# A product of quarters for the sixth of seven products, with its operands kept in DRAM

## The chip, the cores and the metric

The kernel runs on one core of a Trainium2 chip. The time is the device time of one execution in microseconds (us); the median of three runs counts. The engines of a core work side by side, each through its own list of instructions in a fixed order, and wait for each other by semaphores: TensorE (PE; its weight loads are shown as PEld), VectorE (DVE), ScalarE (ACT), GpSimd (POOL) and SyncE (SP). POOL and SP do nothing here but issue DMA transfers. All transfers of the core run on the same 16 DMA engines; SP's requests go through the queue that the profile calls q1, POOL's through q0.

## The reference

```python
def setup_inputs():
    m, k, n = 4096, 4096, 4096
    return {
        "a": np.random.randn(m, k).astype(np.float32),
        "b": np.random.randn(k, n).astype(np.float32),
        "alpha": np.float32(0.01),
    }

def reference(a: np.ndarray, b: np.ndarray, alpha: np.float32) -> np.ndarray:
    x = np.matmul(a, b)
    return np.where(x > 0, x, alpha * x)
```

A product of two 4096 x 4096 matrices and a leaky ReLU on the result.

## The kernel before

**Regions.** The result is cut into 4 x 4 regions of 1024 x 1024. A region (g, j) is group g of rows and block j of columns. The first, (0, 0), is computed plainly while data comes in. The other fifteen are run by the loop at L665, in the order (0, 1), (0, 2), (0, 3), (1, 2), (1, 0), (1, 1), (1, 3), (2, 2), (2, 0), (2, 3), (2, 1), (3, 2), (3, 0), (3, 1), (3, 3). The inputs are rounded to 16-bit floats on their way into the chip's memory (SBUF); sums are kept in 32 bits.

**Seven products instead of eight.** In a region, a's rows and b's columns are each two halves of 512, and the inner dimension two halves of 2048. The 2 x 2 blocks are multiplied by Winograd's form of Strassen's method: seven products (`PRODUCTS`, numbered 0 to 6 in the code) of sums of blocks. They are, in order, a11 b11; a12 b21; s2 t2; s3 t3; s1 t1; a22 (b21 - t2); s4 b22. The texts call a22 (b21 - t2) the sixth and s4 b22 the seventh. s1 to s4 are sums of blocks of a and serve all regions of a group; t1 to t3 are sums of blocks of b, made by VectorE on b's own tiles in each region (`b_sum`, L561). b's tiles are addressed as (half, nt, k): half of the inner dimension, half of the columns, and k, which halves the inner half again. b22 is (1, 1); it enters t2 and t3, and so the operand of the product s2 t2, as the sum `B(0, 1, k) = b22 - b12` and then `B(0, 0, k)`.

A whole product is 64 matmuls of 128 x 128 by 128 x 512 (L680) into four banks of PSUM. PSUM has eight banks; a region uses four as y (products 0, 2, 4, 5 or 6) and four as z. ScalarE copies banks into tiles `c` (`keep`), VectorE adds banks to them (`add`), applies the leaky ReLU (L307), and SP stores them (`leave`, L740).

**A product in quarters.** In nine regions (`in_quarters`: group above 0, not the last of its group) the seventh product is itself cut into 2 x 2 and made of seven products of quarters (`quarters_product`): seven times 16 matmuls of 128 x 128 by 128 x 256 (L711). This needs four sums of quarters of s4 (made once per group by `sums_s4`, kept in DRAM as `kept_s`, and loaded again in the two other regions) and four of b22 (made by VectorE in each region, `sums_b`, L644 to L647).

**Space.** `x_pool` has three slots of 2 MB. s1, s2 and s4 live there; since the sums of quarters need a slot, s2 is given up after its product, comes from DRAM (`kept_s2`) at the region's end, and lies there for the next. s3 overwrites a21 in `a_pool`. `a16_pool` has three slots of 0.5 MB, for a's pieces on their way in, for squares that are measured, and for sums of quarters.

**Loads of b.** Each region's b is 8 MB in 16-bit floats. The next region's tiles go where this region's lie, as soon as the products have read them: `fetch_b(i + 1, ...)` for (0, 1), (0, 0), (1, 0) and (1, 1) in this order, in halves by k, each half by two DMAs of 512 KB from POOL (L505). In the first region of a group b comes from a rounded copy in DRAM, by SP. In the last of a group (`turning`) the next group's a is loaded too (L130) and turned by VectorE (L139).

**Squares.** The kernel measures the sizes of the blocks (`Measure`, placed by `MEASURED` and `EARLY`): ScalarE squares, VectorE adds and folds. At the end this decides whether the fast method's result stands, or all is computed anew.

**Order.** Tiles and their waits are set by the framework; the order on each engine is the order of the code. Places that matter below: `u1 = keep(y, side)` and the four `b_sum` after product 0, `add(u1, z)` after product 1, `in_quarters` after product 3, `add(v, y)` and `leave(v, 1, 1)` after product 4, `product(5, z, False)` with `add(u2, z)`, and `quarters_product` at the end. SP's queue follows the same order: a request whose slot isn't free holds those behind it.

Of the kernel before, what the change touches and what calls it, by code (L numbers as in the profile page):

```python
# [8 lines left out]
P = 128  # L9
DT = mybir.dt.float16  # L10
# [14 lines left out]
KC = 8  # L25
# [6 lines left out]
MT = 4  # L32
# [14 lines left out]
def kernel(  # L47
# [526 lines left out]
    def judge():  # L574
# [26 lines left out]
    B11, B12, B21, B22 = ((1, half, nt) for half in range(2) for nt in range(2))  # L601
    MEASURED = {
        (0, 1): (None, [A11], B12, B11), (0, 2): (B21, [B22, A22], B12, A12),
        (1, 2): (None, [A11], None, None), (1, 0): (B21, [B22, A12], None, None),
        (1, 1): (B21, [B22, A22], None, None),
        (2, 2): (None, [A11], None, None), (2, 0): (A12, [], None, None),
        (2, 3): (B21, [B22, A22], None, None),
        (3, 2): (None, [A11], None, None), (3, 0): (A12, [A22], None, None),
    }


# [3 lines left out]


    HALF = NT // 2
    kept_s = dram_pool.tile([4, P, KC * HALF], DT, name="kept_s")
    kept_s2 = dram_pool.tile([P, 2 * KC * RM], DT, name="kept_s2")
    side = 0  # L620

    def quarter_a(t):
        return t.rearrange("p (c m e) -> p c m e", m=HALF, e=2)

    def rooms(i):

        two = x_pool.tile([P, 2, 2, KC * HALF], DT, name="q", tag="x")
        two = [two[:, 0], two[:, 1]]
        three = [a16_pool.tile([P, KC * HALF], DT, name="sq4", tag="a16") for _ in range(3)]
        tq = {2: two[0][:, 0], 1: two[0][:, 1], 4: two[1][:, 0]}  # L630
        sq = {1: three[0], 2: three[1], 3: three[2], 4: two[1][:, 1]}
        return tq, sq

    def quarters_b(i):
        return {(k, n): have_b[i, 2 + k, 1][:, :, n * HALF:(n + 1) * HALF] for k in range(2) for n in range(2)}

    def quarters_s4(g):
        return {(h, k): s[g, "s4", k][:, :, h * HALF:(h + 1) * HALF, :] for h in range(2) for k in range(2)}

    def sums_b(i, tq):  # L640
        y = quarters_b(i)
        f = lambda n: tq[n].rearrange("p (c n) -> p c n", n=HALF)
        tt = nc.vector.tensor_tensor
        tt(y[0, 1], y[1, 1], y[0, 1], SUB)  # L644
        tt(f(2), y[0, 1], y[0, 0], ADD)
        tt(f(1), y[1, 1], f(2), SUB)
        tt(f(4), y[1, 0], f(2), SUB)  # L647

    def sums_s4(g, sq):
        x = {key: q.rearrange("p c m e -> p c (m e)") for key, q in quarters_s4(g).items()}  # L650
        f = lambda n: sq[n].rearrange("p (c m) -> p c m", m=2 * HALF)
        tt = nc.vector.tensor_tensor
        tt(f(1), x[1, 0], x[1, 1], ADD)
        tt(f(2), f(1), x[0, 0], SUB)
        tt(f(3), x[0, 0], x[1, 0], SUB)
        tt(f(4), x[0, 1], f(2), SUB)
        for n in range(4):
            nc.sync.dma_start(kept_s[n], sq[n + 1])


    def next_a(g, h, half):
# [3 lines left out]
    for i, (g, j) in enumerate(regions):  # L665
# [19 lines left out]
        def new_c(side):  # L685

            pairs = [c_pool.tile([P, 2, NT], FP32, name="c", tag=f"c{side}") for _ in range(2)]
            return pairs, [pairs[mt // 2][:, mt % 2, :] for mt in range(MT)]

        def keep(banks, side):  # L690
            _, kept = new_c(side)
            for mt in range(MT):
                nc.scalar.copy(kept[mt], banks[mt])  # L693
            return kept

        def quarters_product(i, y, acc, other, tq, sq):

            pairs, kept = new_c(side)
            block = lambda r, n: pairs[r][:, :, n * HALF:(n + 1) * HALF]
            b = quarters_b(i)  # L700
            x = quarters_s4(g)
            f = lambda n: tq[n].rearrange("p (c n) -> p c n", n=HALF)
            into = lambda bank: [bank[:, m * HALF:(m + 1) * HALF] for m in range(2)]
            onto = lambda r, n: [y[2 * r + m][:, n * HALF:(n + 1) * HALF] for m in range(2)]
            pair = lambda bank: bank.rearrange("p (m n) -> p m n", m=2)

            def part(xq, yq, to, first=False):
                for c in range(KC):
                    for m in range(2):
                        rows = slice(m * P, (m + 1) * P)  # L710
                        nc.tensor.matmul(  # L711
                            to[m], xq[:, c // 2, rows, c % 2], yq[:, c, :],
                            start=first and (c, m) == (0, 0), stop=c == KC - 1, skip_group_check=True,
                        )

            part(x[0, 1], b[1, 0], onto(0, 0))
            part(x[0, 0], b[0, 0], into(acc), True)
            nc.scalar.copy(block(0, 0), pair(acc))  # L718
            part(quarter_a(sq[4]), b[1, 1], onto(0, 1))
            part(quarter_a(sq[2]), f(2), into(acc))  # L720
            nc.scalar.copy(block(0, 1), pair(acc))
            part(quarter_a(sq[1]), f(1), into(other), True)
            nc.vector.tensor_add(block(0, 1), pair(other), block(0, 1))
            part(quarter_a(sq[3]), b[0, 1], into(acc))
            for n in (1, 0):
                nc.scalar.copy(block(1, n), pair(acc))
            nc.vector.tensor_add(block(1, 1), pair(other), block(1, 1))
            part(x[1, 1], f(4), onto(1, 0))
            for mt in range(MT):
                nc.vector.tensor_add(kept[mt], y[mt], kept[mt])  # L730
            return kept
# [5 lines left out]
        def leave(acc, h, nt):  # L737
            for mt in range(MT):
                leaky(acc[mt])
                nc.sync.dma_start(place(g, h, mt, j, nt), acc[mt])  # L740
# [14 lines left out]
        def fetch_a(h, half, some=slice(None)):  # L755
            if turning:
                for fetch, turn in coming[h, half][some]:
                    fetch()
                    turn()
# [5 lines left out]
        late_ones = [measure(i, *x) for x in late_ones]  # L765
        first_of_group = i == 0 or regions[i - 1][0] != g
        in_quarters = g > 0 and not turning and not final
        early = measure(i, *EARLY[g, j]) if (g, j) in EARLY else None
        if early:
            early.begin()  # L770
        if first_of_group and g:
            nc.sync.dma_start(kept_s2, whole_s[g, "s2"].rearrange("p k c m e -> p (k c m e)"))

        product(0, y, True)
        if early:
            early.end()
        if middle:
            middle.begin()
        u1 = keep(y, side)
        for k in range(2):  # L780
            b_sum(B(0, 1, k), B(1, 1, k), B(0, 1, k), SUB)
            b_sum(B(0, 0, k), B(0, 1, k), B(0, 0, k), ADD)
        if middle:
            middle.end()
        fetch_a(0, 0)

        product(1, z, True)
        add(u1, z)
        if first_of_group:
            sum_a(g, "s3")  # L790
        leave(u1, 0, 0)
        for k in range(2):
            b_sum(B(1, 0, k), B(1, 0, k), B(0, 0, k), SUB)
# [3 lines left out]
        product(2, y, False)  # L797
        if late_ones:
            late_ones[0].begin()
        u2 = keep(y, 1 - side)  # L800
        for k in range(2):
            b_sum(B(0, 0, k), B(1, 1, k), B(0, 0, k), SUB)
        if g:
# [5 lines left out]

        z = [new_bank(zbank + mt) for mt in range(MT)]  # L810
        product(3, z, True)
        v = keep(z, side)
        fetch_b(i + 1, [(0, 1)])
        fetch_a(1, 0)
        for m in late_ones[1:]:
            m.begin()
            m.end()
        if in_quarters:
            tq, sq = rooms(i)
            if first_of_group:  # L820
                sums_s4(g, sq)
            else:
                for n in (4, 2, 1, 3):
                    nc.sync.dma_start(sq[n], kept_s[n - 1])
            if len(late_ones) < 2:
                sums_b(i, tq)

        product(4, y, False)
        a21 = None
        if turning:  # L830
            new_s(g + 1, "s1")
            t = new_s(g + 1, "s2").rearrange("p k c m e -> p (k c m e)").bitcast(BF16)
            a21 = measure(i + 1, 0, 1, 0, t.rearrange("p (n w) -> p n w", n=4))
            a21.begin()
        add(v, y)
        leave(v, 1, 1)
        if in_quarters and len(late_ones) == 2:
            sums_b(i, tq)
        if a21:
            a21.end()  # L840
        if fifth:
# [4 lines left out]
        if final:  # L846
            good = judge()

        product(5, z, False)
        fetch_b(i + 1, [(1, 0)])  # L850
        add(u2, z)
        fetch_a(1, 1, slice(3))
        leave(u2, 1, 0)
        if sixth:
# [6 lines left out]
                sum_a(g + 1, name)  # L861

        if in_quarters:
            kept_c = quarters_product(i, y, new_bank(zbank + 2), new_bank(zbank + 3), tq, sq)
            fetch_b(i + 1, [(1, 1)])
            t = new_s(g, "s2")
            nc.sync.dma_start(t.rearrange("p k c m e -> p (k c m e)"), kept_s2)
            leave(kept_c, 0, 1)
        else:
            product(6, y, False)  # L870
            fetch_b(i + 1, [(1, 1)])
            if final:
                even = nc.values_load(good[0:1, 0:1], min_val=0, max_val=1)
            _, kept_c = new_c(side)

            def store(mt):
                nc.sync.dma_start(place(g, 0, mt, j, 1), kept_c[mt])

            for mt in range(MT):
                nc.scalar.copy(kept_c[mt], y[mt])  # L880
                leaky(kept_c[mt])
                if not (final and mt == MT - 1):
                    store(mt)
# [69 lines left out]
```

## Time and profile before

| what | value |
|---|---|
| median of 3 runs | 1567.9 us (1567.63 to 1568.17) |
| the profiled execution | 1567.84 us |
| its span in the profile | 1565.9 us |
| granted TensorE clock | 0.999 |
| instructions in the profile | 19332 |
| moved by DMA | 291.84 MB, 186 GB/s over the span |

The profile is of one execution. Its page gives each engine's busy time and share of the span, DMA queues with packets, megabytes and the time that their packets took as a share of 16 engines' span, and the costliest groups of instructions. Other views give the instructions in order of time (start, length, engine, line, operation, output and inputs, and in brackets the idle time before and what ended it) and the busy time by stage. A DMA share over 1 means that packets overlapped on the engines. Regions start, by PE's timeline, at 412.93 (1, 2), 508.03 (1, 0), 603.14 (1, 1), 698.25 (1, 3), 794.94 (2, 2), 890.05 (2, 0), 985.15 (2, 3), 1080.26 (2, 1), 1176.95 (3, 2), 1272.06 (3, 0), 1367.16 (3, 1) and 1462.27 (3, 3).

### The profile page before, as it was taken

To read this page: it belongs to the slowest core of one execution; us is meant where nothing else is said; L and a number is where in the kernel's file an instruction comes from. 1 tells how busy PE (TensorE), PEld (TensorE's weight loads), DVE (VectorE), ACT (ScalarE), POOL (GpSimd) and SP (SyncE) were. 2 spreads that over 40 slices of the span, in tenths; PEclk is the share of its full clock that TensorE was granted. 3 is DMA by queue.
4 is the path that set the end of the run, shared out by engine and by line. 5 is a ranking of instruction groups with operands and counts; after the bars stand their busy time and mean duration, and the time that the engine had idled before them with its cause. 6 is when DMAs were issued, how large, how long until landed. Compare 5 with 4: busy or idle time off the path is not lost. (4 is left out here: it accounts for less than half of the span.)

```text
span 1565.9 us, 19332 instructions
## 1 busy us (share of the span) xinstructions
PE 1554.8 (99%) x7707; PEld 753.0 (48%) x7707; DVE 1055.6 (67%) x1172; ACT 372.4 (24%) x390; POOL 299.7 (19%) x482
## 2 busy tenths in 40 slices
PE   9999999999999999999999999999999999999998
PEld 4444444444445445454444545545444454544543
DVE  4378758767975776766789682774868959372533
ACT  2201243612120334401221220531022143110110
POOL 5641110244002011023401102012330110201100
PEclk9999999999999999999999999999999999999999
DMA  9999795999829589499975949769995793949902
GB/s 244 186 217 185 151 279 150 190 194 203 284 54 246 157 167 237 92 249 209 183 275 114 276 135 174 176 140 276 168 235 203 170 260 96 217 144 193 210 27 84
DMA packets 199142, 291.84 MB, mean 186 GB/s; under 512 B 17281, under 2 KB 154753, under 8 KB 193666
## 3 DMA queue, kind: packets, MB, share of 16 engines
q0 software_dynamic: 149376, 141.59, 57.4%
q1 hardware_dynamic: 49378, 148.53, 25.4%
q8 instruction: 62, 1.02, 0.3%
q10 hardware_dynamic: 288, 0.39, 0.1%
q14 instruction: 38, 0.31, 0.1%
HBM read 341.84 MB, written 88.08 MB: 275 GB/s over the span
## 5 line engine op out<-in xcount | busy, mean ns | idle before, releaser
L680 PE MATMUL ps<-b,a 128*128 128x512 f16 x3840 | 836.1, 379 | 0.0
L680 PEld LDWEIGHTS <-a 128*128 128x128 f16 x3840 | 375.7, 98 | 451.1
L680 PE MATMUL ps<-b,s 128*128 128x512 f16 x2304 | 503.2, 379 | 0.0
L680 PEld LDWEIGHTS <-s 128*128 128x128 f16 x2304 | 225.4, 98 | 271.9
L561 DVE TENSOR_TENSOR b<-b 128x4096 f16<-128x4096 f16 x112 | 252.8, 2290 | 94.9 <-DMA b<-in_b_dram 80.0
L505 POOL DMA_DIRECT2D b<-in_b_dram x184 | 136.3, 746 | 940.9 <-PE ps L680 635.7
L735 DVE TENSOR_TENSOR c<-ps,c 128x512 f32<-128x512 f32 x180 | 111.6, 683 | 168.4 <-PE ps L680 110.1
L693 ACT COPY c<-ps 128x512 f32<-128x512 f32 x180 | 92.3, 598 | 538.5 <-PE ps L680 431.0
L139 DVE STREAM_TRANSPOSE a<-a 128x512 uint32<-128x512 uint32 (+2 forms) x120 | 126.3, 1101 | 90.5 <-DMA a<-in_a_dram 89.8
L130 POOL DMA_DIRECT2D a<-in_a_dram x252 | 137.5, 553 | 196.5 <-DVE a L139 122.5
L307 DVE SCALAR_TENSOR_TENSOR c<-c 128x512 f32<-128x512 f32 x240 | 149.5, 686 | 12.7 <-ACT c L880 10.0
L227 ACT ACTIVATE sq<-b 128x2048 bf16<-128x2048 f16 x64 | 119.1, 1910 | 89.8 <-DVE sq L236 75.8
L279 PE MATMUL ps<-b,a 128*128 128x512 f16 x512 | 112.8, 379 | 2.1 <-DMA b<-in_b_dram 0.9
L227 ACT ACTIVATE sq<-a 128x2048 bf16<-128x2048 f16 x48 | 88.8, 1921 | 77.2 <-DVE sq L236 60.3
L279 PEld LDWEIGHTS <-a 128*128 128x128 f16 x512 | 49.7, 98 | 63.0 <-issue 2.9
L718 ACT COPY c<-ps 128x512 f32<-128x512 f32 x9 | 5.3, 586 | 244.2 <-PE ps L711 244.2
L236 DVE TENSOR_TENSOR sq<-sq 128x2048 bf16<-128x2048 bf16 x27 | 33.0, 1223 | 28.8 <-ACT sq L227 28.8
L711 PEld LDWEIGHTS <-s 128*128 128x128 f16 x432 | 42.2, 98 | 6.8
L239 DVE TENSOR_TENSOR sq<-sq 128x2048 bf16<-128x2048 bf16 x27 | 33.1, 1225 | 17.2 <-ACT sq L227 17.2
L711 PEld LDWEIGHTS <-sq 128*128 128x128 f16 x432 | 42.3, 98 | 4.8
L238 DVE TENSOR_TENSOR sq<-sq 128x2048 bf16<-128x2048 bf16 x27 | 33.1, 1226 | 4.7 <-ACT sq L227 2.3
L880 ACT COPY c<-ps 128x512 f32<-128x512 f32 x24 | 12.6, 598 | 98.0 <-PE ps L680 98.0
(86 smaller groups left out, 559.7 us busy)
## 6 DMA issues: line engine op xcount, KB each, us to landing
b<-in_b_dram POOLq DMA_DIRECT2D x192, 512.0 KB, 10.5
out_dram<-c SPq DMA_DIRECT2D x240, 256.0 KB, 6.5
a<-in_a_dram POOLq DMA_DIRECT2D x244, 128.0 KB, 5.5
b<-kept SPq DMA_DIRECT2D x24, 1024.0 KB, 8.5
s<-kept_s SPq DMA_DIRECT2D x9, 2048.0 KB, 10.4
sq<-kept_s SPq DMA_DIRECT2D x18, 512.0 KB, 7.1
b<-in_b_dram POOLq DMA_DIRECT2D x24, 256.0 KB, 9.2
kept<-b SPq DMA_DIRECT2D x6, 1024.0 KB, 7.7
```

The costliest lines, as they stand in the source:

```text
L130: nc.gpsimd.dma_start(a16[32 * q:32 * q + 32], src.rearrange("(g i) w -> i g w", i=32))
L139: nc.vector.transpose(part.rearrange("p c m e -> p c (m e)").bitcast(U32) .rearrange("p c (g i) -> p g c i", i=32), src[:, :, i * n:(i + 1 ...
L227: nc.scalar.activation(to, self.parts[n], SQUARE)
L238: nc.vector.tensor_add(total, total, more[1])
L279: nc.tensor.matmul(ps, a_cols(at[0, h, u], c, mt, (h, u) == (0, 0)), bt[0, u, nt][:, c, :], start=first, stop=last,)
L307: nc.vector.scalar_tensor_tensor(t, t, alpha, t, op0=MULT, op1=MAX if alpha <= 1 else MIN)
L505: nc.gpsimd.dma_start(t[:, c:c + 4, :], b_rows(j, u, c, 4, nt, g > 0))
L561: nc.vector.tensor_tensor(f(to), f(x0), f(x1), op)
L680: nc.tensor.matmul(banks[mt], a_cols(t, c, mt, t is first_a), B(half, nt, k)[:, c, :], start=first and (k, c) == (0, 0), stop=(k, c) == (1 ...
L693: nc.scalar.copy(kept[mt], banks[mt])
L711: nc.tensor.matmul(to[m], xq[:, c // 2, rows, c % 2], yq[:, c, :], start=first and (c, m) == (0, 0), stop=c == KC - 1, skip_group_check=True,)
L735: nc.vector.tensor_add(acc[mt], banks[mt], acc[mt])
```

## The change

In six regions, those `in_quarters` that are not the first of their group (`both`: (1, 0), (1, 1), (2, 0), (2, 3), (3, 0), (3, 1)), the sixth product is formed from seven products of quarters as well. The space for its sums is made by keeping s1 and s3 in DRAM too, beside s2: they are written in the group's first region, given up in each of the six, and loaded again at its end. a22's sums of quarters are made in the group's first region and kept in DRAM. Where the sixth product was added into z, on top of s3 t3, it now has banks of its own, and v (a copy of z) is added to u2 before. The blocks whose squares are measured are dealt out to other regions.

```diff
     MEASURED = {
         (0, 1): (None, [A11], B12, B11), (0, 2): (B21, [B22, A22], B12, A12),
-        (1, 2): (None, [A11], None, None), (1, 0): (B21, [B22, A12], None, None),
-        (1, 1): (B21, [B22, A22], None, None),
-        (2, 2): (None, [A11], None, None), (2, 0): (A12, [], None, None),
-        (2, 3): (B21, [B22, A22], None, None),
+        (1, 0): (A12, [B22], None, None), (1, 1): (A22, [A11], None, None),
+        (2, 0): (B21, [A12], None, None), (2, 3): (A22, [A11], None, None),
         (3, 2): (None, [A11], None, None), (3, 0): (A12, [A22], None, None),
+        (3, 1): (B21, [B22], None, None), (3, 3): (B21, [B22], None, None),
     }
...
-    kept_s = dram_pool.tile([4, P, KC * HALF], DT, name="kept_s")
-    kept_s2 = dram_pool.tile([P, 2 * KC * RM], DT, name="kept_s2")
+    QUARTER = KC * HALF
+    kept_s = {name: dram_pool.tile([P, 2 * KC * RM], DT, name=f"kept_{name}") for name in ("s1", "s2", "s3")}
+    kept_q = {name: dram_pool.tile([4, P, QUARTER], DT, name=f"kept_q{name}") for name in ("a22", "s4")}
...
+    def load_sums(name, to, which):
+        for n in which:
+            nc.sync.dma_start(to[n], kept_q[name][n - 1])
+
+    def quarter_product(xq, yq, to, first=False):
+        for c in range(KC):
+            for m in range(2):
+                rows = slice(m * P, (m + 1) * P)
+                nc.tensor.matmul(
+                    to[m], xq[:, c // 2, rows, c % 2], yq[:, c, :],
+                    start=first and (c, m) == (0, 0), stop=c == KC - 1, skip_group_check=True,
+                )
...
+    def load_s(g, name):
+        if name == "s3":
+            for k in range(2):
+                t = s[g, name, k] = a_pool.tile([P, KC // 2, RM, 2], DT, name="s3", tag="a21")
+                nc.sync.dma_start(t.rearrange("p c m e -> p (c m e)"), kept_s[name][:, k * KC * RM:(k + 1) * KC * RM])
+        else:
+            t = new_s(g, name)
+            nc.sync.dma_start(t.rearrange("p k c m e -> p (k c m e)"), kept_s[name])
...
+        def sixth_in_quarters(pairs, banks, tq, sq, w):
+            b = quarters_of_b(i, 1, 0)
+            x = quarters_of_a(g, "a22")
+            one, other, third, fourth = banks
...
+            quarter_product(x[0, 0], b[0, 0], into(one), True)
+            nc.scalar.copy(w[0], one)
+            quarter_product(sx(1), t(1), into(other), True)
+            more(1, 1, other)
+            quarter_product(x[0, 1], b[1, 0], into(fourth), True)
+            quarter_product(sx(2), t(2), into(one))
+            nc.scalar.copy(w[1], one)
+            quarter_product(x[1, 1], t(4), into(third), True)
+            quarter_product(sx(3), b[0, 1], into(one))
+            quarter_product(sx(4), b[1, 1], into(other))
+            yield
+            more(0, 0, fourth)
+            more(0, 0, w[0])
+            more(0, 1, w[1])
+            more(1, 0, third)
+            more(1, 0, one)
+            more(1, 1, one)
+            more(0, 1, other)
...
         in_quarters = g > 0 and not turning and not final
+        both = in_quarters and not first_of_group
...
         if in_quarters:
-            tq, sq = rooms(i)
-            if first_of_group:
-                sums_s4(g, sq)
-            else:
-                for n in (4, 2, 1, 3):
-                    nc.sync.dma_start(sq[n], kept_s[n - 1])
-            if len(late_ones) < 2:
-                sums_b(i, tq)
+            t = x_pool.tile([P, 4, QUARTER], DT, name="q", tag="x")
+            tq, sq = {2: t[:, 0], 1: t[:, 1], 4: t[:, 2]}, {4: t[:, 3]}
+        if both:
+            for n in (1, 2, 3):
+                sq[n] = new_a16()
+            load_sums("a22", sq, (1, 2, 3, 4))
+            sums_of_b(quarters_of_b(i, 1, 0), tq)
+            tq6, sq6 = tq, sq
+            t = [a_pool.tile([P, 2, QUARTER], DT, name="q", tag="a21") for _ in range(2)]
+            tq, sq = {2: t[0][:, 0], 1: t[0][:, 1], 4: t[1][:, 0]}, {4: t[1][:, 1]}
+            sums_of_b(quarters_of_b(i, 1, 1), tq)
+            for mt in range(MT):
+                nc.vector.tensor_add(u2[mt], u2[mt], v[mt])
...
         product(4, y, False)
...
+        if both:
+            t = x_pool.tile([P, 4, QUARTER], DT, name="q", tag="x")
+            for n in (1, 2, 3):
+                sq[n] = t[:, n - 1]
+            load_sums("s4", sq, (4, 2, 1, 3))
+            w = t[:, 3].bitcast(FP32)
+            w = [w[:, :NT], w[:, NT:]]
         add(v, y)
+        if both:
+            rest = sixth_in_quarters(u2_pairs, [new_bank(zbank + mt) for mt in range(MT)], tq6, sq6, w)
+            next(rest)
         leave(v, 1, 1)
...
-        product(5, z, False)
+        if both:
+            for _ in rest:
+                pass
+            load_s(g, "s2")
+        else:
+            product(5, z, False)
+            add(u2, z)
         fetch_b(i + 1, [(1, 0)])
-        add(u2, z)
         fetch_a(1, 1, slice(3))
         leave(u2, 1, 0)
...
-            kept_c = quarters_product(i, y, new_bank(zbank + 2), new_bank(zbank + 3), tq, sq)
+            kept_c = seventh_in_quarters(y, new_bank(zbank + 2), new_bank(zbank + 3), tq, sq)
             fetch_b(i + 1, [(1, 1)])
-            t = new_s(g, "s2")
-            nc.sync.dma_start(t.rearrange("p k c m e -> p (k c m e)"), kept_s2)
+            if not both:
+                load_s(g, "s2")
             leave(kept_c, 0, 1)
+            if both:
+                load_s(g, "s3")
+                load_s(g, "s1")
```

`sums_of_a`, `sums_of_b` and `seventh_in_quarters` do what `sums_s4`, `sums_b` and `quarters_product` did, for any operand. `keep_s` writes s1, s2 or s3 to DRAM; `into(bank)` gives the two halves of a bank, and `more` adds a bank or a copy of one to a quarter of u2.

## The prediction

> **What bounds the kernel now.** I read the page first (busy shares, then the DMA queues), the timeline of PE, the busy time by stage of one region, VectorE's timeline at the start of the next, and the DMA queues in a short window. The chain of waits holds only the last store's preparation (0.7 us) and tells nothing.
>
> ```profile
> PE 1554.8 (99%) x7707; PEld 753.0 (48%) x7707; DVE 1055.6 (67%) x1172; ACT 372.4 (24%) x390; POOL 299.7 (19%) x482
> ...
> q0 software_dynamic: 149376, 141.59, 57.4%
> q1 hardware_dynamic: 49378, 148.53, 25.4%
> ```
>
> PE is busy from end to end, and no line of PE's timeline after the start-up has idle time before it. So the time is the sum of the products until something makes PE wait. q1 (SP's queue: stores and everything that comes back from DRAM) moved 148.53 MB in 25.4% of 1565.9 us, 397.7 us: 373 GB/s. A block of 2.10 MB (s1, s2 or s3) costs all 16 engines 5.6 us.
>
> ```profile
> 481.99 13.98 PE L680 MATMUL ps<-b,a 128*128 128x512 f16 x64
> 495.81 3.66 PE L711 MATMUL ps<-b,s 128*128 128x256 f16 x32
> ...
> 508.03 12.25 PE L680 MATMUL ps<-b,a 128*128 128x512 f16 x56
> ```
>
> Start to start (first column), a whole product takes 495.81 - 481.99 = 13.82 us (64 matmuls, 216 ns each) and one in quarters 508.03 - 495.81 = 12.22 us (112, 109 ns each).
>
> The stages of region (1, 0), which is one of the six that change; the columns are the stage, its length, PE, PEld, DVE, ACT and POOL busy, the clock, DMA share and GB/s:
>
> ```profile
> 521.85:535.66 13.81, 13.81 (x65) 6.27 (x64) 11.42 (x7) 3.51 (x5) 0.00 (x0) 1.00 0.39 74
> 535.66:549.47 13.81, 13.81 (x65) 6.27 (x64) 13.64 (x19) 5.96 (x4) 0.00 (x0) 1.00 0.20 76
> 549.47:563.29 13.82, 13.82 (x66) 6.26 (x65) 9.80 (x12) 3.97 (x6) 1.48 (x2) 1.00 0.53 103
> 563.29:577.10 13.81, 13.81 (x65) 6.24 (x64) 7.09 (x10) 8.80 (x8) 2.97 (x4) 1.00 0.98 154
> 577.10:590.91 13.81, 13.81 (x65) 6.27 (x64) 9.61 (x13) 0.00 (x0) 2.96 (x4) 1.00 1.12 284
> 590.91:603.14 12.23, 12.23 (x113) 10.96 (x112) 6.07 (x11) 2.72 (x5) 4.23 (x6) 1.00 1.20 243
> ```
>
> The DMA engines are nearly free for two stages and full in the last two (577 to 603), where the next region's b arrives. How late that is shows on VectorE at the start of the next region, (1, 1), which begins at 603.14:
>
> ```profile
> 617.58 2.29 DVE L561 TENSOR_TENSOR b<-b 128x4096 f16<-128x4096 f16 x1 [2.77 <-DMA b<-in_b_dram]
> 620.33 2.29 DVE L561 TENSOR_TENSOR b<-b 128x4096 f16<-128x4096 f16 x1 [0.46 <-DVE b L561]
> 623.23 4.69 DVE L561 TENSOR_TENSOR b<-b 128x4096 f16<-128x4096 f16 x2 [0.61 <-DMA b<-in_b_dram]
> ```
>
> VectorE waits for b's last block, b22: its first half is there 14.4 us into the region, its second at 20.1. Two sums of 2.29 us on each half make the operand of product 2, which starts at 2 x 13.81 = 27.6 us. So the first half has 27.6 - 4.6 - 14.4 = 8.6 us to spare.
>
> Last, who gets the engines when both queues have work. The first line is from 604 to 607 us, the others from 607.2 to 612, when s2's 2 MB come back:
>
> ```profile
> q0 software_dynamic: 607, 0.61, 121.3%
> ```
> ```profile
> q1 hardware_dynamic: 110, 1.80, 90.0%
> q0 software_dynamic: 108, 0.11, 13.4%
> ```
>
> 110 packets against 108: they alternate, but q1's hold 16 KB and q0's 1 KB. b's loads fall from 0.61 MB in 3 us (203 GB/s) to 0.11 MB in 4.8 us (23 GB/s).
>
> **The change, part by part.**
>
> *Sixth product, six times.* Six whole products become six in quarters: the built program has 48 more matmuls for each, 288 in all. 6 x (13.82 - 12.22) = **-9.6 us**. The Trainium skill (TensorE: Matmul & The Clock Gate, section Back-to-back issue gap) gives a sustained spacing of 131 ns at 512 columns and 81 at 128; as an estimate from that page, 64 x 131 = 8.4 us against at least 112 x 81 = 9.1, the split would cost 0.7 us each time and the term would be +4.2. The trace disagrees with 216 and 109 ns, so this gets no chance.
>
> *VectorE and ScalarE.* Each of the six regions gets four sums of quarters of b (1.22 us by L644 to L647: 4.9 us), four additions of v to u2, and seven additions of quarters where four additions of 0.60 (L735, start to start) were. The addition of v has both inputs in SBUF, as none in the trace: from 0.60 to 0.69 (the mean of L307, also f32 there). I take 0.69 for it and the seven: 4.9 + 2.8 + 4.8 - 2.4 = 10.1 us. Region (1, 0) would use 62.5 + 10.1 of 93.5 us. Groups 1 to 3 measure the squares of fifteen blocks (by `MEASURED`) before and after, dealt out differently. What hides this: VectorE idles 6.7 and 4.2 us in the stages at 563 and 577. Inside the sixth, the last deadline is the bank that the seventh's second quarter takes, 12.22 + 1.75 = 14.0 us after the sixth begins. VectorE has by then 4 x 0.6 (v), 0.7, 4 x 0.6 (leaky) and four quarter additions, the last once quarter five has ended (8.7 + 0.3): about 9.7 us. Cost 0; 4.3 us to spare, and each us beyond would cost 6. ScalarE's two copies of 0.59 have two quarters' time (3.5 us).
>
> *Writes of s1, s3 and a22's sums*, 6.3 MB in three regions: SP's queue in the first stages, DMA share 0.2 to 0.4. Cost 0; they stand in front of no b load (uncovered, 17 us in each of three).
>
> *Loads.* Each of the six gets s1 and s3 (4.19 MB) at its end, a22's four sums (2.10 MB) from product 3 on, and s4's sums move: one early, three (1.57 MB) to the sixth's start, since they go where s1 lay. s2 comes after the sixth, not the seventh. On SP's queue s2 waits for the sixth's end and s1 and s3 for the seventh's; behind s2 stand only stores, behind s3 and s1 nothing until the next region's first stores. All lie ahead of or among b22's loads, on engines that are full from the sixth's start to 622. So I add their time to b22's landing. Low: s1 and s3 alone, 4.19 / 0.373 = 11.2 us. High: with the three sums, 15.4. (Below nothing is excluded: more bytes bring nothing earlier.) Before, the first half was there 617.58 - 577.10 = 40.5 us after the sixth began; now 51.7 to 55.9. The next region begins after two products in quarters, 24.4: 27.3 to 31.5 into it. Two sums: 31.9 to 36.1, where product 2 is due at 27.6. **A wait of 4.3 to 8.5 us, in each of six regions**; I take the middle, 6.4, as I see no row that tells how much of the three sums finds room: +38.4. The second half, 5.65 us later, is summed just as PE comes to it (6.9 us into product 2).
>
> *What is late next.* In the turning regions (1, 3) and (2, 1) VectorE turns the next group's a between those sums and u1's addition, which frees the banks of product 3 (due at 739.69):
>
> ```profile
> 732.55 2.10 DVE L139 STREAM_TRANSPOSE a<-a 128x512 uint32<-128x512 uint32 x2 [2.94 <-DMA a<-in_a_dram]
> 734.58 2.44 DVE L735 TENSOR_TENSOR c<-ps,c 128x512 f32<-128x512 f32 x4
> ```
>
> The addition ends at 737.02, 2.7 us early. b22's second half moves 13.0 us within the region at the low end, product 3 by 4.3: 8.7 - 2.7 = 6.0 late if the 2.94 us of waiting for a stays, 3.1 if it is absorbed, 0 if a's loads catch up. I take 3, twice: +6.
>
> **Sum**: 1567.84 (the profiled execution: span 1565.9 and 1.9 around it; the median is 1567.9) - 9.6 + 38.4 + 6 = **1602.6 us**.
>
> **Rivals.**
> *b keeps its rate (faster).* If s1 and s3 took only time in which b's loads don't need the engines, the first half would land by 23.0 into the region and PE would not wait (up to 24.6 the wait stays under the 1.6 us gained, which is the point from which it decides). For: the engines are idle soon after 623 (share 0.39 in a second stage). Against: 23 GB/s beside a 16 KB stream; the first half has 8.6 us to spare, less than 11.2. Time: 1567.8 - 9.6 = 1558.2.
> *A short wait.* The three sums find room, and a third of s1 falls behind b22: 11.2 - 1.9 = 9.3, a wait of 2.4: 1567.8 - 9.6 + 14.4 = 1572.6; with a wait of 4, 1582. For: the stage at 563 has room (share 0.98, with overlapping packets counted twice). Against: s1's packets take nearly all of an engine once they come.
> *VectorE too becomes late.* The wait for b22 holds the squares, u1's addition and the stores behind it in all six regions, not two: 3 us each, 18, and the high end of the wait (8.5): 1567.8 - 9.6 + 51 + 18 = 1627. For: squares of b or a stand between sums and addition in most of them. Against: in (1, 1) that addition ended at 637.4, 12 us before product 3.
>
> **How the numbers follow.** Forecast 0.66, short wait 0.14, VectorE late 0.13, faster 0.07. Range: the forecast's own is 1567.8 - 9.6 + 25.8 = 1584 to 1567.8 - 9.6 + 51 + 12 = 1621; I reach into the short wait, 1578, and to 1624. A measurement of this kernel tells about 0.2% (3 us) from nothing: faster by more 0.07, within 0.02 (the edge of the short wait), slower 0.91.
>
> **What would show it.** Sixth products of 12.2 us in six regions; gaps of 4 to 9 us on PE just before product 2 of (1, 1), (1, 3), (2, 3), (2, 1), (3, 1) and (3, 3), ended by VectorE's L561, itself ended by a load of b; smaller gaps before product 3. Wrong, if PE has no gaps there, if b22 lands under 23 us into a region, or if gaps stand inside the sixth or seventh.

## The result, and the profile after

The changed kernel takes 1624.46 us (median of 4 runs, 1621.91 to 1626.67) against 1568.04 for the kernel before: 1.0359 times as long, 95% interval 1.0341 to 1.0377. The profiled execution took 1623.82 us, its span is 1622.0. Forecast were 1602.6 us and a range up to 1624.0: the kernel became slower, as forecast, but the loss is 56 us instead of 35, and the time lies just above the range.

The page of the changed kernel, engines' busy time, DMA queues, and the two groups of whole products (busy time and mean, then idle time before them and what ended it):

```profile
PE 1561.5 (96%) x7995; PEld 784.0 (48%) x7995; DVE 1129.2 (70%) x1256; ACT 380.3 (23%) x402; POOL 299.6 (18%) x482
...
q0 software_dynamic: 149376, 141.59, 54.6%
q1 hardware_dynamic: 59314, 205.16, 33.2%
...
L717 PE MATMUL ps<-b,a 128*128 128x512 f16 x3072 | 670.7, 380 | 7.5 <-DMA b<-in_b_dram 7.5
L717 PE MATMUL ps<-b,s 128*128 128x512 f16 x2688 | 597.3, 384 | 40.4 <-DVE b L561 36.2
```

PE now has idle time, 36.2 us of it ended by VectorE's sums of b (L561). q1 moved 205 MB instead of 149, q0 the same as before. PE's timeline from the sixth product of region (1, 0) on:

```profile
577.23 1.91 PE L668 MATMUL ps<-b,a 128*128 128x256 f16 x16
...
589.45 3.66 PE L668 MATMUL ps<-b,s 128*128 128x256 f16 x32
...
601.68 27.79 PE L717 MATMUL ps<-b,a 128*128 128x512 f16 x128
636.11 29.25 PE L717 MATMUL ps<-b,s 128*128 128x512 f16 x124 [6.64 <-DVE b L561]
```

The sixth and the seventh take 12.22 and 12.23 us, without a gap. Products 0 and 1 of region (1, 1) run from 601.68 to 629.3; then PE stands for 6.6 us. VectorE at this place, and the DMA queues from 614 to 620 us:

```profile
630.93 2.29 DVE L561 TENSOR_TENSOR b<-b 128x4096 f16<-128x4096 f16 x1 [17.59 <-DMA b<-in_b_dram]
633.67 6.99 DVE L561 TENSOR_TENSOR b<-b 128x4096 f16<-128x4096 f16 x3 [0.46 <-DVE b L561]
```
```profile
q1 hardware_dynamic: 255, 1.96, 80.4%
q0 software_dynamic: 257, 0.25, 24.6%
```

b22's first half is there 29.2 us into the region instead of 14.4. While s3 and s1 come, the two queues take turns by packets (255 and 257), and b gets 0.25 MB of 2.21. After the wait the clock is not what it was. The stages around it (the last three columns are granted clock, DMA share and GB/s):

```profile
622.30:629.30 7.00, 7.00 (x34) 3.04 (x31) 0.00 (x0) 0.00 (x0) 0.00 (x0) 1.00 1.10 287
629.30:636.11 6.81, 0.17 (x1) 0.03 (x1) 4.72 (x3) 0.00 (x0) 0.00 (x0) 0.85 0.95 158
636.11:640.85 4.74, 4.74 (x12) 1.67 (x13) 4.64 (x3) 0.00 (x0) 0.00 (x0) 0.50 0.00 0
640.85:650.00 9.15, 9.15 (x44) 4.17 (x43) 8.26 (x13) 6.88 (x4) 0.00 (x0) 1.00 0.00 0
```

From 636.11 to 640.85 PE does 12 matmuls in 4.74 us, at half the clock. And two more places of waiting, from PE's timeline in the regions (1, 3) and (3, 3):

```profile
730.51 3.61 PE L717 MATMUL ps<-b,a 128*128 128x512 f16 x16 [1.85 <-DMA b<-in_b_dram]
740.56 15.28 PE L717 MATMUL ps<-b,s 128*128 128x512 f16 x64 [6.44 <-DVE b L561]
757.63 0.38 PE L717 MATMUL ps<-b,s 128*128 128x512 f16 x1 [1.79 <-DVE c L792]
...
1531.38 8.75 PE L717 MATMUL ps<-b,a 128*128 128x512 f16 x32 [4.04 <-DMA b<-in_b_dram]
1543.92 16.37 PE L717 MATMUL ps<-b,s 128*128 128x512 f16 x75 [3.79 <-DVE b L561]
```

The two lines ended by a load of b stand inside product 1, which reads b21 in order: in (1, 3) 16 of its 64 matmuls are left and b21's last DMA is missing, in (3, 3) 32 are left and its second half is. Adding up every gap between matmuls over its usual spacing gives the whole account:

| where | us | forecast |
|---|---|---|
| matmuls themselves (six sixths in quarters) | -9.4 | -9.6 |
| wait before product 2, six regions (6.8, 6.6, 6.6, 6.5, 6.7, 4.0) | +37.2 | +38.4 |
| wait before product 3, turning regions | +5.4 | +6 |
| wait inside product 1 (2.0, 0.8, 1.2, 4.2) | +8.2 | none |
| matmuls at half the clock | +12.6 | none |
| from the last matmul to the end, 9.2 us instead of 7.2 | +2.0 | none |
| sum (spans: 1622.0 - 1565.9 = 56.1) | +56.0 | +34.8 |

### The profile page after: what moved, and what is told of

Its sections match the earlier page's. It is cut to its first block, busy times and chain, and to the rows that moved or that the text cites. A ratio compares the mean times of both kernels' runs of the same rounds, so it can differ in the third digit from the quotient of the medians.

```text
span 1622.0 us, 20146 instructions
## 1 busy us (share of the span) xinstructions
PE 1561.5 (96%) x7995; PEld 784.0 (48%) x7995; DVE 1129.2 (70%) x1256; ACT 380.3 (23%) x402; POOL 299.6 (18%) x482
## 5 line engine op out<-in xcount | busy, mean ns | idle before, releaser
L717 PE MATMUL ps<-b,a 128*128 128x512 f16 x3072 | 670.7, 380 | 7.5 <-DMA b<-in_b_dram 7.5
L717 PE MATMUL ps<-b,s 128*128 128x512 f16 x2688 | 597.3, 384 | 40.4 <-DVE b L561 36.2
L717 PEld LDWEIGHTS <-a 128*128 128x128 f16 x3072 | 301.1, 98 | 369.9 <-issue 11.0
L717 PEld LDWEIGHTS <-s 128*128 128x128 f16 x2688 | 265.2, 99 | 368.5 <-issue 60.0
L561 DVE TENSOR_TENSOR b<-b 128x4096 f16<-128x4096 f16 x112 | 252.7, 2291 | 182.9 <-DMA b<-in_b_dram 174.6
L730 ACT COPY c<-ps 128x512 f32<-128x512 f32 x180 | 92.2, 597 | 447.4 <-PE ps L717 366.0
L792 DVE TENSOR_TENSOR c<-ps,c 128x512 f32<-128x512 f32 x156 | 96.6, 682 | 65.5 <-PE ps L717 37.2
L279 PE MATMUL ps<-b,a 128*128 128x512 f16 x512 | 112.9, 379 | 2.1 <-DVE part L318 0.9
L668 PEld LDWEIGHTS <-q 128*128 128x128 f16 x960 | 93.9, 98 | 10.9
L279 PEld LDWEIGHTS <-a 128*128 128x128 f16 x512 | 49.7, 98 | 63.1 <-issue 3.4
L668 PE MATMUL ps<-b,q 128*128 128x256 f16 x480 | 56.3, 273 | 0.0
L239 DVE TENSOR_TENSOR sq<-sq 128x2048 bf16<-128x2048 bf16 x27 | 33.1, 1225 | 17.4 <-ACT sq L227 17.4
L668 PEld LDWEIGHTS <-s 128*128 128x128 f16 x432 | 42.3, 98 | 5.5
L780 DVE TENSOR_TENSOR c<-ps,c 128x512 f32<-128x512 f32 x9 | 6.2, 692 | 47.0 <-issue 47.0
L775 ACT COPY c<-ps 128x512 f32<-128x512 f32 x9 | 5.3, 586 | 131.7 <-PE ps L668 131.7
L236 DVE TENSOR_TENSOR sq<-sq 128x2048 bf16<-128x2048 bf16 x27 | 33.0, 1223 | 4.2 <-ACT sq L227 4.2
## 6 DMA issues: line engine op xcount, KB each, us to landing
b<-in_b_dram POOLq DMA_DIRECT2D x192, 512.0 KB, 14.4
```

Of the source, the lines that this page charges most:

```text
L239: nc.vector.tensor_add(total, total, self.held[3])
L279: nc.tensor.matmul(ps, a_cols(at[0, h, u], c, mt, (h, u) == (0, 0)), bt[0, u, nt][:, c, :], start=first, stop=last,)
L561: nc.vector.tensor_tensor(f(to), f(x0), f(x1), op)
L668: nc.tensor.matmul(to[m], xq[:, c // 2, rows, c % 2], yq[:, c, :], start=first and (c, m) == (0, 0), stop=c == KC - 1, skip_group_check=True,)
L717: nc.tensor.matmul(banks[mt], a_cols(t, c, mt, t is first_a), B(half, nt, k)[:, c, :], start=first and (k, c) == (0, 0), stop=(k, c) == (1 ...
L792: nc.vector.tensor_add(acc[mt], banks[mt], acc[mt])
```

## The experiments

Theory A: the loads of s1, s3 and s4's sums stand on full DMA engines ahead of b's last tiles. Theory B: the sixth in quarters frees those tiles later, so their loads are issued later. Theory C: VectorE's added work makes the sums late.

**Without the loads of s1 and s3.**

```diff
             if both:
-                load_s(g, "s3")
-                load_s(g, "s1")
+                for k in range(2):
+                    s[g, "s3", k] = operand(g, "a12", k)
+                    s[g, "s1", k] = s[g, "s4", k]
```

> The changed kernel without the loads of s1 and s3 at the end of the six regions; in the regions after them the products take a12 in place of s3 and s4 in place of s1, so these two products have other operands, and PE has as many matmuls. Theory A (bytes on full DMA engines push b's last tile back): the first half of b22 is 11 us or more earlier, the wait before product 2 goes from 6.8 us to none in all six, with it the half clock and the wait in product 1; 1558 to 1566 us. Theory B (the sixth in quarters frees b21's and b22's tiles later, so their loads are issued later): issue times stay, waits of 4 us or more stay, about 1610 to 1624. Theory C (VectorE's added work makes the sums late): no change, 1624.

1563.65 us, 0.9972 (0.9963 to 0.9982) of before. VectorE in region (1, 1), which begins at 602.88 here:

```profile
622.26 2.29 DVE L561 TENSOR_TENSOR b<-b 128x4096 f16<-128x4096 f16 x1 [7.72 <-DMA b<-in_b_dram]
```

b22's first half is there at 19.4 us instead of 29.2, early enough. PE's products 0 and 1, and product 2 behind them:

```profile
602.88 27.79 PE L717 MATMUL ps<-b,a 128*128 128x512 f16 x128
630.50 13.98 PE L717 MATMUL ps<-b,s 128*128 128x512 f16 x64
```

In all six regions there is no wait before product 2, none in product 1, and no half clock. Theory A holds: the quarters and VectorE's added work are still there, so theories B and C alone don't make these waits. The loads of s1 and s3 delay b22 by 9.9 us (the forecast's low end was 11.2). Left are 4.2 us of waits before product 3 in the turning regions.

**Without s4's sums too.**

On top of the edit above:

```diff
...
-            load_sums("s4", sq, (4, 2, 1, 3))
+            sq = None
...
+            if sq is None:
+                x4 = quarters_of_a(g, "s4")
+                sq = {1: x4[1, 0], 2: x4[1, 1], 3: x4[0, 0], 4: x4[0, 1]}
```

> The changed kernel without the loads of s1 and s3 (the products after it take a12 and s4 in their place) and without the loads of s4's four sums of quarters in the six regions (the seventh's quarters take s4's own quarters). Without s1 and s3 alone b22's first half lands 19.3 us into region (1, 1), against 14.3 in the kernel before. Theory A (bytes): 1.57 MB less from the sixth's start, 4 us earlier: 15 to 16, second half 20 to 21. If the 5 us come from the sixth in quarters freeing b21's and b22's tiles later, they stay: 19.

1560.03 us in one run; b22's halves land 16.0 and 21.0 us into region (1, 1). So s4's sums are worth 3.3 of the remaining 5.0 us. The other 1.7 are no delay: the shorter sixth brings the region's start forward by 1.6 us. Counted from the sixth's start, b22's first half lands after 40.4 us in the kernel before, 53.6 in the changed kernel, 43.7 without s1 and s3, and 40.5 here. In this region nothing that can be measured is left for theory B.

**The loads alone**, in the kernel before: s1 and s3 are written to DRAM in each group's first region, and

```diff
...
             leave(kept_c, 0, 1)
+            if not first_of_group:
+                reload(g)
```

reloads them in place in the same six regions.

> The kernel before with nothing of the sixth product changed, but s1 and s3 written to DRAM in each group's first region and loaded into their own places again (same data) at the end of the same six regions, behind the stores of the seventh product. Theory A: b22's first half lands about 11 us later, 25 to 26 us into the region, its sums end at 30 to 31 where product 2 is due at 27.6: waits of 2 to 4 us, with half clock 2 us more, and in the turning regions a wait before product 3; 1585 to 1605. Theories B and C (nothing of the quarters is there): 1568.

1588.59 us, 1.0130 (1.0113 to 1.0147). The time is in the range, the place is not. VectorE in region (1, 1), from 602.27:

```profile
616.59 4.69 DVE L561 TENSOR_TENSOR b<-b 128x4096 f16<-128x4096 f16 x2 [2.66 <-DMA b<-in_b_dram]
632.28 4.69 DVE L561 TENSOR_TENSOR b<-b 128x4096 f16<-128x4096 f16 x2 [11.01 <-DMA b<-in_b_dram]
```

The first half is as early as before (14.3 us), having got through ahead of s3; only the second is late, 30.0 instead of 20.1. Product 2 hardly waits (1.5 us in all); the late sums hold u1's addition, and product 3 waits for its banks, 15.5 us over four regions, with 4.5 us of half clock. The loads alone cost 20.7 us with nothing more in quarters than before. In the changed kernel both halves of b22 fall behind them; s4's sums, which push b back by 3.3 us ahead of s3, have a part in that, and what the earlier load of s2 adds was not measured.

**Less work on VectorE.** Left out: `sums_of_b` for the sixth, the additions of v, and five of the eight calls of `more` (the expectation counts six of nine, the prediction seven where there are eight).

> The changed kernel with most of VectorE's added work left out: the four sums of quarters of b for the sixth product (its quarters take b's own quarters in their place), the four additions of v to u2 and six of the nine additions to u2's quarters (the first to (1, 1), and those that free the third and fourth bank, stay); the block u2 is then not the reference's. Transfers are the same. Theory A: the waits before product 2 stay at 6.5 to 6.8 us, 1620 to 1627. Theory C (VectorE's added 10 us a region makes the sums late): the waits shrink by several us each, under 1600.

1623.57 us in one run. VectorE and PE in region (1, 1), from 603.00:

```profile
631.55 4.69 DVE L561 TENSOR_TENSOR b<-b 128x4096 f16<-128x4096 f16 x2 [16.89 <-DMA b<-in_b_dram]
```
```profile
636.38 13.84 PE L717 MATMUL ps<-b,s 128*128 128x512 f16 x53 [5.60 <-DVE b L561]
```

The load still ends VectorE's wait, and PE waits 5.6 here and 6.5 to 6.9 in the others. Theory C falls here too.

**Zeros where PE waited.**

```diff
...
+        if i and g and not first_of_group and was_both:
+            for n in range(32):
+                nc.tensor.matmul(y[n % MT], w0[:, :P], w0, start=False, stop=False, skip_group_check=True)
         product(2, y, False)
```

> The changed kernel with 32 matmuls of zeros by zeros (128 columns of weights, 512 moving, adding 0 to y's banks) ahead of product 2 in each of the six regions after those with the sixth in quarters: 32 x 0.216 = 6.9 us that PE spends where it waited. If the slow matmuls after each wait (0.43 us instead of 0.216, granted clock 0.5) come from PE's idleness, the clock stays at 1.0, the wait is no longer than 1 us and the time falls by most of the 12.6 us: 1611 to 1615. If the half clock has another cause, it stays, and the time is 1624 or up to 6 x 3 us above.

1619.88 us, 1.0325 (1.0307 to 1.0342). The stages in region (1, 1), as above:

```profile
629.30:636.20 6.90, 6.74 (x32) 3.03 (x31) 4.96 (x3) 0.00 (x0) 0.00 (x0) 1.00 0.84 140
636.20:641.00 4.80, 4.80 (x24) 2.15 (x22) 4.70 (x3) 0.00 (x0) 0.00 (x0) 1.00 0.00 0
```

The clock stays at 1.00 and PE does 24 matmuls where it did 12. So idleness halved it: half-clock time falls from 12.6 to 4.5 us, what is left standing behind other waits. The time fell by less than expected (1611 to 1615). The zeros take 41 us where the waits were 37, and product 2, now at full speed, ends earlier while VectorE doesn't: product 3's waits in the turning regions grow from 5.4 to 8.8 us.

**s3 and s1 through POOL's queue.** Same bytes, behind b22's loads on one queue:

```diff
-                nc.sync.dma_start(t.rearrange("p c m e -> p (c m e)"), kept_s[name][:, k * KC * RM:(k + 1) * KC * RM])
+                nc.gpsimd.dma_start(t.rearrange("p c m e -> p (c m e)"), kept_s[name][:, k * KC * RM:(k + 1) * KC * RM])
...
-            nc.sync.dma_start(t.rearrange("p k c m e -> p (k c m e)"), kept_s[name])
+            queue = nc.gpsimd if name == "s1" else nc.sync
+            queue.dma_start(t.rearrange("p k c m e -> p (k c m e)"), kept_s[name])
```

> The changed kernel with one difference: the loads of s3 and s1 at the end of the six regions go through POOL's queue, right behind b22's loads, and no longer through SP's. Same bytes, same products. Theory A with turns taken by packets: b22's first half lands 20 to 22 us into the region instead of 29, the second 25 to 27, s3 at 33 to 35 (due at 41.4), s1 at 38 to 40 (due at 55); no wait before product 2 and no half clock after it. In the two turning regions a's pieces are now behind s3 and s1 on the same queue, 11 us later than before, and VectorE stands at them before it frees product 3's banks: a wait of 5 to 10 us there with half clock, twice. 1568 to 1582 us. If the number of bytes alone decided, whatever the queue, b22 would land at 29 us again: 1624.

1583.78 us, 1.0105 (1.0077 to 1.0132), just above the expected 1568 to 1582: 41 us are won by the queue on which the same loads stand. The queues from 617 to 623 us show b alone, and VectorE in region (1, 1), from 601.8, begins its sums in time; in the turning region (1, 3) PE waits before product 3:

```profile
q0 software_dynamic: 1228, 1.22, 123.2%
```
```profile
621.06 2.29 DVE L561 TENSOR_TENSOR b<-b 128x4096 f16<-128x4096 f16 x1 [7.60 <-DMA b<-in_b_dram]
```
```profile
747.65 12.72 PE L718 MATMUL ps<-b,s 128*128 128x512 f16 x43 [10.74 <-DVE c L793]
```

No wait before product 2 is left. The two turning regions have 12.0 and 9.9 us before product 3, counted as in the table, since a's pieces queue behind s3 and s1: VectorE stands 9.0 us at one of them in (1, 3). Region (3, 2), which follows the second, waits 2.0.

**Turning a after u1's addition** in groups 1 and 2, on top of the change of queue:

```diff
-        fetch_a(0, 0)
+        if not g:
+            fetch_a(0, 0)
 
         product(1, z, True)
         add(u1, z)
+        if g:
+            fetch_a(0, 0)
```

> As the run with POOL's queue and six regions, with VectorE's turning of the next group's a moved behind u1's addition in groups 1 and 2. Theory A: product 3's banks are free in time, what remains is s1's or a's lateness further on in the two turning regions, waits of 0 to 4 us each: 1560 to 1570. If the wait in the turning regions comes from the bytes themselves (the DMA share is 1.01 there before the change) and not from VectorE's order, the time is that of the run with POOL's queue.

1574.58 us, 1.0045 (1.0029 to 1.0060), where 1560 to 1570 were expected. Product 3 no longer waits, so VectorE's order was 9 us of the loss; but product 4 does, 4.2 and 3.0 us in the profiled execution (1569.19), and the runs spread from 1569 to 1576. Bytes and order both have a part in the turning regions.

**Four regions instead of six**: the sixth stays whole ahead of a turning region, the loads go through POOL's queue.

```diff
...
-        both = in_quarters and not first_of_group
+        both = in_quarters and not first_of_group and not (i + 2 < len(regions) and regions[i + 2][0] != g)
```

Regions (1, 1) and (2, 3) load s4's sums ahead of product 4, as the kernel before did.

> As the run before with POOL's queue, but the sixth product stays whole in the two regions ahead of a turning one, (1, 1) and (2, 3), and no s1 and s3 are loaded there; four regions have it in quarters. Theory A: no wait anywhere, four times 1.6 us are gained: 1561 to 1564, or 1560 if all is hidden. If quarters in the sixth cost something else (VectorE, ScalarE, PSUM), waits of 1 us or more remain in these four regions and the time is 1566 or more.

1561.42 us (1560.72 to 1562.31), 0.9959 (0.9945 to 0.9972): a little faster than the kernel before, by 0.4%. Its page, with the idle time of the whole products last:

```profile
PE 1549.0 (99%) x7899; PEld 771.9 (50%) x7899; DVE 1109.2 (71%) x1232; ACT 378.2 (24%) x398; POOL 306.1 (20%) x494
...
L718 PE MATMUL ps<-b,a 128*128 128x512 f16 x3200 | 696.4, 379 | 0.0
L718 PE MATMUL ps<-b,s 128*128 128x512 f16 x2688 | 585.1, 379 | 0.0
```

PE has no wait after the start-up. The gain is 6.7 us, where 4 x 1.6 = 6.4 were due.

## Where the prediction was right, and the step that failed

*The gain* (-9.6) and *VectorE and ScalarE at nothing* held: -9.4 us, no gap in the sixth or seventh, and no change with VectorE's additions gone.

*Loads.* The mechanism and its place were right: b22's first half was to land 27.3 to 31.5 us into the region and landed at 29.2; the wait of 6.4 us was 6.8, 6.6, 6.6, 6.5, 6.7 and 4.0. That the middle was met so closely is in part luck. It was taken because no row told how much of s4's three sums finds room; in the runs they count in full, but both parts are smaller than priced: 9.9 us instead of 11.2 for s1 and s3 and 3.3 instead of 4.2 for the sums, 13.2 in all, where the middle of 11.2 and 15.4 is 13.3.

*What is late next.* The turning regions came out as costed, 5.4 for 6. But this step looked only at what comes after b22. b21's second half, on the same queue ahead of it, is read from 20.7 us into the region on, in the second half of product 1, and was late too in four regions: 8.2 us that the sum lacks. The step failed by following the last tile and not every tile that the full engines delay.

*The sum* is the step that failed most: it priced each wait at its length and put nothing down for the clock. The five waits of 6.5 us or more, and one of 4.2, also halved the clock of the matmuls behind them, 12.6 us in all. In the kernel before PE never idles after the start-up, so its trace could show slow matmuls only there (L103 takes 572 ns on average, L680 379); the zeros show the cause.

*Rivals.* The faster one (b keeps its rate) is refuted by 0.25 MB in 6 us while s3 and s1 come, the short wait by waits of 6.5 us and more. *VectorE too becomes late* names 1627 us, near the measured time, but not for its reason: outside the turning regions no wait stands before product 3 in the changed kernel. The argument against it was weaker than it looks, though: u1's addition in (1, 1) ended 7.2 us before product 3 was due (603.14 + 3 x 13.81 = 644.6), not 12, and with the loads alone product 3 of (1, 1) does wait, 1.9 us.

The 2.0 us after the last matmul stay unexplained. They are there with the zeros and with less work on VectorE too (9.2 and 9.3 us), and in no other run (7.2 to 7.4).

## What to carry to other kernels

When a change adds transfers, look which stage they fall into and what is due soonest behind them: the same bytes cost 41 us more on one queue than on another, where they stood behind the urgent loads. Four of the six regions then started without a wait, and leaving the other two as they were made the change a small gain. Follow every tile that a full DMA stage delays, not just the last. And a wait of TensorE costs more than its length if it loses the clock.

## What the runs showed of the hardware

**The clock after a wait.** The half-clock stretches in the changed kernel last 6.83 us four times, 10.24 and 3.41: multiples of 3.41 us. Waits of 6.5 to 6.8 and of 4.2 us brought one, waits of 2.0 and less none, and neither did the 4.0 at 1543.92. The Trainium skill (TensorE: Matmul & The Clock Gate, section What's actually happening) tells of a free-running window of 3.4 us: a window without work halves the clock, one full of work restores it. The lengths agree. That a window has to be without work doesn't: in the run with zeros a wait of 2.1 us in region (3, 3) (1528.2 to 1530.3) was followed by one stretch at half the clock, 1530.9 to 1534.3, and PE had been busy for 1.44 us of the 3.41 before it. The wait of 4.0 lies across two windows of this length, counted on from the stretch before, with 1.58 and 1.45 us of work in them, and lost nothing. So the place of a wait counts beside its length; where the limit lies no run here settles.

**Two queues take turns by packets, whatever their size.** 255 packets against 257 while s3 and s1 come, with 1.96 MB against 0.25: packets of 8 KB on average leave a load that rounds on its way, in packets of 1 KB, a ninth of the bytes. While stores in packets of 2 KB run (608 to 614 us) it is 590 against 590, with 1.18 MB against 0.59. With all on one queue, in order of issue, b moved 1.22 MB in 6 us.
